# Zero columns added to the matmuls of layer 0, a different number for each weight group, and one projection summed at other PSUM columns

## The chip, the core and the metric

The kernel runs as one program on one core of one Trainium2 chip. The metric is device time in microseconds (us) of one execution. Before the change two executions took 2308.03 and 2309.26 us, a median of 2308.65. A third execution, recorded by the hardware profiler, took 2307.92 us; its span from the first to the last instruction is 2306.1 us.

## What is computed

A decoder trunk of two layers over 272 tokens (16 learned prefix tokens and a sequence of 256), width 2048, 16 heads of 128, feed-forward width 8192, all in fp32. Layer 0 mixes tokens with forgetting attention, layer 1 with stick-breaking attention over one shared K/V. What matters here are the dense products; in the reference they are:

```python
h = jnp.concatenate([meta, x], axis=1)                    # 272 tokens
a = rms_norm(h, norm_attn[0])
proj = a @ fox_w_in[0]                                    # q, k, v, forget gates
h = h + o.reshape(b, length, D_MODEL) @ fox_w_o[0]        # o: forgetting attention
h = h + squared_relu_mlp(rms_norm(h, norm_mlp[0]), w_up[0], w_down[0])
a = rms_norm(h, norm_attn[1])
c = rms_norm(h, kv_norm)
k_s, v_s = jnp.split(c @ w_kv, 2, axis=-1)                # shared K/V, all 272 tokens
q = split_heads(a @ sb_w_q[0])
h = h + o.reshape(b, length, D_MODEL) @ sb_w_o[0]         # o: stick-breaking attention
h = h + squared_relu_mlp(rms_norm(h, norm_mlp[1]), w_up[1], w_down[1])
return rms_norm(h, final_norm)[:, N_META:]
```

## The kernel before

**Layout.** Activations lie feature-major: 16 chunks of 128 features on the partitions, tokens along the free axis. A layer-0 product works on 272 tokens, and so does the shared K/V projection; the rest of layer 1 works on the 256 tokens behind the prefix.

**A split operand.** Every dense product is made from fp32r matmuls. Each operand is split into a high part, which fp32r holds, and a low part with the remainder, and three products are summed: weight-high by x-high, weight-high by x-low, weight-low by x-high. The class `Split` allocates the x tile: per chunk 640 columns, with the high part starting at a column given by `ROWS` and the low part 320 columns behind it. The start is column 48 for the 272-token tiles and column 0 for the 256-token tiles. The pool `xs` holds two such tiles, so a new tile waits for the last reader of the one whose place it takes.

**A weight group.** `gemm_group` multiplies x by a 2048 x 512 block of weights. It allocates four PSUM tiles `acc` of one bank each (512 fp32 columns), one for each block m of 128 output features. The reduction runs in four steps kb of four chunks kc. For each kb two weight halves are loaded by SyncE's DMA queue, ScalarE writes the high part (`whi`, line 219) and VectorE the low part (`wlo`, line 220). Then come 48 matmuls per kb, 192 per group, each with a weight load of its own, all recorded at line 179 in the helper `gemm_matmul`. In layer 0 the order inside a kb is block by block (or in halves of a kb), and for each chunk the three products follow one another. In layer 1 the order is product by product across the blocks, and three of a group's 192 matmuls are 262 columns wide instead of 256: they read `sp.wide`, which goes six columns beyond x into zeros that GpSimd wrote from the tile `pad` (line 132).

**The groups in order.** They are numbered u by the order in which the code makes them: 1 to 12 are q, k and v of layer 0 in four rounds of four heads, 13 to 16 the output projection of layer 0, 17 to 48 its MLP, 49 to 52 the queries of layer 1, 53 to 60 the shared K/V, 61 to 64 the output projection of layer 1 and 65 to 96 its MLP. An MLP runs in four quarters f of the hidden width: four up groups that read `x_m` and write the quarter's hidden tile `x_u`, then four down groups that read that tile. For layer 0 this makes u = 17 + 8f + g, with g from 0 to 3 for the up groups and from 4 to 7 for the down groups.

**What sets the order.** A scheduler that simulates a timeline places the instructions on each engine's queue. Within the dense products the order of the matmuls is pinned by explicit dependencies from one to the next, except in the first group, whose x arrives piece by piece. The attention matmuls of a round are slotted between those of the next group. Each engine works through its queue in order.

**Lines.** `ROWS` and `Split` (lines 27 and 118 to 132), `gemm_group` (185 to 251), the matmul call (247) and the evacuation call (251). In attention, lines 295 and 296 multiply x by the 32 columns of the gate weights, 427 to 429 transpose probabilities into columns 0, 128 and 256 of one PSUM tile, 447 and 448 transpose packed values that GpSimd prepared at lines 338 and 345, and 588 to 593 are fp32r matmuls of 512 and 288 columns.

Of the kernel before, what the change touches and what calls it, by code (L numbers as in the profile page):

```python
# [15 lines left out]
P = 128  # L16
D = 2048
NC = D // P
M = 16
# [4 lines left out]
QSCALE = 1.0 / math.sqrt(P)  # L24
N_FF = 4

ROWS = {0: (48, 368), M: (0, 320)}
XROW = 640

G_A0, G_M0, G_KV, G_A1, G_M1, G_FIN = range(6)  # L30
# [3 lines left out]
def yoco_kernel(ctx: ExitStack, tc: tile.TileContext, hT_in, gains, b_f, w_f, w_qkv0, w_o0, w_up, w_dn,  # L34
                w_kv, w_q1, w_o1, outT):
    nc = tc.nc
# [77 lines left out]
    pad = align.tile([P, 32], F32, name="pad")  # L114
# [3 lines left out]
    class Split:  # L118


        def __init__(self, label, t0):
            n = T - t0
            self.t0 = t0
            rows = xs.tile([P, NC * XROW + 64], F32R, tag="x", name=f"x_{label}")
            hi, lo = ROWS[t0]
            rows = rows[:, hi:hi + NC * XROW].rearrange("p (c t) -> p c t", c=NC)
            d = lo - hi
            self.hi, self.lo = rows[:, :, :n], rows[:, :, d:d + n]
            if t0:

                self.wide = rows[:, :, :n + 6]
                nc.gpsimd.tensor_copy(rows[:, :, n:n + 6], pad[:, :6].unsqueeze(1).to_broadcast([P, NC, 6]))

    def split_chunk(sp, gi, c):

        g = g_sb[:, gi, c:c + 1]
        nc.scalar.activation(sp.hi[:, c], hT[:, c, sp.t0:], AF.Copy, scale=g)
        nc.vector.scalar_tensor_tensor(out=sp.lo[:, c], in0=hT[:, c, sp.t0:], scalar=g,
                                       in1=sp.hi[:, c].bitcast(F32), op0=ALU.mult, op1=ALU.subtract)
# [37 lines left out]
    def gemm_matmul(*args, **kw):  # L177

        ins = nc.tensor.matmul(*args, **kw).ins  # L179
        if queued and pinned[0]:  # L180
            tc.add_manual_dep(ins, queued[0].name, mybir.DependencyInfo(mybir.DependencyClass.NoSync,
                                                                        mybir.DependencyReason.DATA))
        queued[:] = [ins]

    def gemm_group(wblk, sp, t0, evac, before={}, after={}, load_x=None):

        uid[0] += 1
        u = uid[0]  # L190
        accs = [pacc.tile([P, 512], F32, tag="acc", name=f"acc_{u}_{m}") for m in range(4)]
        n = T - t0
        for kb in range(4):
            src_w = wblk[kb].rearrange("p (k c) -> p k c", k=4)
            if kb in before:
                before[kb]()
            piece = 1 if load_x is not None and kb < 2 else 2
            raws = [wraw.tile([P, 2, 512], F32, tag="raw", name=f"raw_{u}_{kb}_{hf}") for hf in range(2)]
            for k0 in range(0, 4, piece):
                if load_x is not None:  # L200
                    load_x(range(4 * kb + k0, 4 * kb + k0 + piece))
                if load_x is not None and kb == k0 == 0:

                    for c0 in (0, 256):
                        nc.scalar.dma_start(raws[0][:, 0, c0:c0 + 256], src_w[:, 0, c0:c0 + 256])
                else:
                    nc.sync.dma_start(raws[k0 // 2][:, k0 % 2:k0 % 2 + piece], src_w[:, k0:k0 + piece])
            parts = []
            for hf in range(2):
                whi, wlo = (wspl.tile([P, 2, 576], F32R, tag=f"w{x}", name=f"w{x}_{u}_{kb}_{hf}") for x in ("hi", "lo"))  # L210
                o = 16 if t0 else 0
                whi, wlo = whi[:, :, o:o + 512], wlo[:, :, o:o + 512]
                boxes = [(o, piece, 0, 512) for o in range(0, 2, piece)]
                if load_x is not None and kb == hf == 0:
                    boxes[:1] = [(0, 1, 0, 256), (0, 1, 256, 512)]
                for o, no, c0, c1 in boxes:
                    src = raws[hf][:, o:o + no, c0:c1]
                    hp, lp = whi[:, o:o + no, c0:c1], wlo[:, o:o + no, c0:c1]
                    on_act = nc.scalar.activation(hp, src, AF.Copy)  # L219
                    on_dve = nc.vector.tensor_tensor(out=lp, in0=src, in1=hp.bitcast(F32), op=ALU.subtract)  # L220
                parts.append((whi, wlo))
            if kb in after:
                with tc.issue_after(on_act.ins), tc.issue_after(on_dve.ins):
                    after[kb]()

            if load_x is not None and kb == 0:
                runs = [([kc], range(4)) for kc in range(4)]
            elif kb in (0, 3):
                runs = [(range(4), [m]) for m in range(4)]
            else:  # L230
                runs = [(range(2 * hf, 2 * hf + 2), range(4)) for hf in range(2)]
            pinned[0] = load_x is None
            for kcs, ms in runs:
                pairs = ((0, sp.hi), (0, sp.lo), (1, sp.hi))
                if t0:
                    products = [(kc, m, *pair) for pair in pairs for kc in kcs for m in ms]
                else:
                    products = [(kc, m, *pair) for m in ms for kc in kcs for pair in pairs]
                left = {m: 3 * len(kcs) for m in ms}

                wide = [(0, 0, 0), (1, 0, 1), (2, 1, 1)] if t0 else []
                for kc, m, part, x in products:
                    first, left[m] = kb == kc == 0 and left[m] == 3 * len(kcs), left[m] - 1
                    nw = n
                    if m == 3 and x is sp.hi and (kb, kc, part) in wide:
                        x, nw = sp.wide, n + 6
                    gemm_matmul(accs[m][:, :nw], parts[kc // 2][part][:, kc % 2, m * P:(m + 1) * P], x[:, 4 * kb + kc],
                                start=first, stop=kb == kc == 3 and left[m] == 0)
                if kb == 3:
                    for m in ms:  # L250
                        evac(m, accs[m][:, :n])

    def residual_add(c, acc, t0):
        nc.vector.tensor_tensor(out=hT[:, c, t0:], in0=acc, in1=hT[:, c, t0:], op=ALU.add)  # L254
# [6 lines left out]
    def load_x(chunks):  # L261
        c0, n = chunks[0], len(chunks)
        nc.sync.dma_start(hT[:, c0:c0 + n, :], hT_in[:, c0:c0 + n, :])
        if c0 == 0:
            nc.sync.dma_start(g_sb, gains)
        for c in chunks:
            split_chunk(xa, G_A0, c)
# [86 lines left out]
    for g in range(4):  # L354
# [11 lines left out]
        if g == 0:  # L366

            gemm_group(w_qkv0[0], xa, 0, lambda m, acc, qT=qT: nc.scalar.copy(qT[:, m, :], acc),
                       after={kb: (lambda kb=kb: first_norm(kb)) for kb in range(4)}, load_x=load_x)
            gate_products()  # L370
            box["rstd"] = norm.finish()
            for m in range(4):
                evac_q(m, qT[:, m, :])
            forget_gates(box["rstd"])
        else:
            gemm_group(w_qkv0[3 * g], xa, 0, evac_q)
# [4 lines left out]
        def decays(j):  # L381

            for i, (o, n) in enumerate(((0, 144), (144, T))):
                nc.vector.scalar_tensor_tensor(out=s[:, j, o:o + n], in0=fk[:, j, :n],
                                               scalar=fq_sb[:, i, 4 * g + j:4 * g + j + 1],
                                               in1=maskA[:, o:o + n], op0=ALU.subtract, op1=ALU.add)

        gemm_group(w_qkv0[3 * g + 1], xa, 0, lambda m, acc: evac_kv(m, acc, kT),
                   after={j: (lambda j=j: decays(j)) for j in range(4)})

# [263 lines left out]
    for i in range(2):  # L654
        pr = patt.tile([P, 512], F32, tag="patt", name=f"pr_fin_{i}")
        for b in range(2):
            nc.tensor.matmul(pr[:, b * P:(b + 1) * P], rs[:, b:b + 1].to_broadcast([P, P]), ident,
                             start=True, stop=True)
# [67 lines left out]
```

## Time and profile before

| what | value |
|---|---|
| median of two executions | 2308.65 us |
| profiled execution, its own time | 2307.92 us |
| its span, first to last instruction | 2306.1 us |
| TensorE clock granted, mean over the span | 0.998 of full |
| VectorE busy | 1290.2 us, 56% |
| ScalarE busy | 1041.7 us, 45% |
| GpSimd busy | 42.4 us, 2% |
| read from HBM | 407 MB, 178 GB/s over the span |

A row of the profile's groups gives line, engine, operation, output and inputs, the shape (stationary size, then output), a count, busy time, and the mean duration of one instruction. Matmuls overlap in a pipeline, so the mean duration of one (281 ns for most dense matmuls) is longer than the time from its start to the next one's start. That time is called the step in what follows, and it is read from rows of the timeline or of a window: the difference of two start times, divided by the matmuls started between them.

### The profile page before, as it was taken

To read this page: it belongs to the slowest core of one execution; us is meant where nothing else is said; L and a number is where in the kernel's file an instruction comes from. 1 tells how busy PE (TensorE), PEld (TensorE's weight loads), DVE (VectorE), ACT (ScalarE), POOL (GpSimd) and SP (SyncE) were. 2 spreads that over 40 slices of the span, in tenths; PEclk is the share of its full clock that TensorE was granted. 3 is DMA by queue.
4 is the path that set the end of the run, shared out by engine and by line. 5 is a ranking of instruction groups with operands and counts; after the bars stand their busy time and mean duration, and the time that the engine had idled before them with its cause. 6 is when DMAs were issued, how large, how long until landed. Compare 5 with 4: busy or idle time off the path is not lost.

```text
span 2306.1 us, 44831 instructions
## 1 busy us (share of the span) xinstructions
PE 2294.4 (99%) x19030; PEld 2281.9 (99%) x19030; DVE 1290.2 (56%) x1764; ACT 1041.7 (45%) x1397; POOL 42.4 (2%) x65
## 2 busy tenths in 40 slices
PE   9999999999999999999999999999999999999998
PEld 9999999999999999999999999999999999999998
DVE  7665555655455455455566555566555555555554
ACT  6444344543344344345444444455543543543553
POOL 1010000000000000000000000000000000000000
PEclk9999999999999999999999999999999999999999
DMA  7544445555555555555556444456556556566563
GB/s 239 169 156 167 166 165 167 172 183 177 180 174 181 180 171 186 177 181 170 186 180 200 161 144 146 146 167 199 186 192 203 186 195 201 184 201 197 188 200 130
DMA packets 116648, 412.32 MB, mean 179 GB/s; under 512 B 13264, under 2 KB 16736, under 8 KB 116448
## 3 DMA queue, kind: packets, MB, share of 16 engines
q1 hardware_dynamic: 114560, 406.29, 52.9%
q8 instruction: 149, 2.44, 0.4%
q10 hardware_dynamic: 1888, 3.16, 0.4%
q14 instruction: 51, 0.42, 0.1%
HBM read 407.29 MB, written 2.11 MB: 178 GB/s over the span
## 4 chain that ended last, share of the span: by engine, by line
PE 99%; DVE 0%; DMA 0%; ACT 0%; SPq 0%; issue 0%; DVEq 0%; ACTq 0%
PE acc L179 95%; PE ps L396 0%; PE pza L573 0%; PE pv L329 0%; PE po L458 0%; PE po L612 0%; DMA raw<-w_qkv 0%; PE po L613 0%; PE pzb L574 0%; PE po L459 0%; PE po L614 0%; DVE ob L668 0%; PE pf L295 0%; PE pf L296 0%; PE pta L588 0%; PE pta L589 0%
## 5 line engine op out<-in xcount | busy, mean ns | idle before, releaser
L220 DVE TENSOR_TENSOR wlo<-raw,whi 128x1024 fp32r<-128x1024 f32 (+1 forms) x773 | 928.2, 1217 | 752.6 <-ACT whi L219 745.9
L219 ACT ACTIVATE whi<-raw 128x1024 fp32r<-128x1024 f32 (+1 forms) x773 | 796.5, 1050 | 999.0 <-PE acc L179 984.3
L179 PE MATMUL acc<-x_m,whi 128*128 128x272 f32 (+1 forms) x4096 | 643.1, 281 | 0.0
L179 PE MATMUL acc<-x_u,whi 128*128 128x272 f32 (+1 forms) x4096 | 643.0, 281 | 0.0
L179 PEld LDWEIGHTS acc<-x_m,whi 128*128 128x128 f32 x4096 | 566.1, 188 | 0.1
L179 PEld LDWEIGHTS acc<-x_u,whi 128*128 128x128 f32 x4096 | 566.0, 188 | 0.0
L179 PE MATMUL acc<-x_u,wlo 128*128 128x272 f32 (+2 forms) x2048 | 440.8, 281 | 0.0
L179 PE MATMUL acc<-x_m,wlo 128*128 128x272 f32 (+2 forms) x2048 | 440.8, 281 | 0.0
L179 PE MATMUL acc<-x_a,whi 128*128 128x272 f32 (+1 forms) x2048 | 359.6, 288 | 0.7 <-ACT whi L219 0.6
L179 PEld LDWEIGHTS acc<-x_m,wlo 128*128 128x128 f32 x2048 | 323.3, 188 | 0.0
L179 PEld LDWEIGHTS acc<-x_u,wlo 128*128 128x128 f32 x2048 | 323.3, 188 | 0.0
L179 PEld LDWEIGHTS acc<-x_a,whi 128*128 128x128 f32 x2048 | 301.3, 188 | 2.9 <-ACT whi L219 0.8
L179 PE MATMUL acc<-x_a,wlo 128*128 128x272 f32 (+2 forms) x1024 | 253.7, 285 | 0.0
L179 PE MATMUL acc<-x_kv,whi 128*128 128x272 f32 x1024 | 194.1, 288 | 0.0
L179 PEld LDWEIGHTS acc<-x_a,wlo 128*128 128x128 f32 x1024 | 175.6, 188 | 0.7 <-issue 0.5
L179 PE MATMUL acc<-x_o,whi 128*128 128x272 f32 (+1 forms) x1024 | 162.3, 282 | 0.0
L179 PEld LDWEIGHTS acc<-x_kv,whi 128*128 128x128 f32 x1024 | 160.6, 188 | 0.4
L179 PE MATMUL acc<-x_kv,wlo 128*128 128x272 f32 x512 | 147.3, 288 | 0.0
L179 PEld LDWEIGHTS acc<-x_o,whi 128*128 128x128 f32 x1024 | 142.0, 188 | 0.1
L254 DVE TENSOR_TENSOR hT<-acc,hT 128x272 f32<-128x272 f32 (+1 forms) x160 | 69.1, 432 | 84.8 <-PE acc L179 84.6
L179 PE MATMUL acc<-x_o,wlo 128*128 128x272 f32 (+2 forms) x512 | 110.6, 282 | 0.0
L179 PEld LDWEIGHTS acc<-x_kv,wlo 128*128 128x128 f32 x512 | 96.5, 188 | 0.1
(225 smaller groups left out, 972.4 us busy)
## 6 DMA issues: line engine op xcount, KB each, us to landing
raw<-w_up SPq DMA_DIRECT2D x256, 512.0 KB, 4.6
raw<-w_dn SPq DMA_DIRECT2D x256, 512.0 KB, 4.5
raw<-w_qkv SPq DMA_DIRECT2D x92, 512.0 KB, 3.7
raw<-w_o SPq DMA_DIRECT2D x64, 512.0 KB, 4.2
raw<-w_kv SPq DMA_DIRECT2D x64, 512.0 KB, 3.8
raw<-w_q SPq DMA_DIRECT2D x32, 512.0 KB, 4.8
fk<-f_dram ACTq DMA_DIRECT2D x4, 544.0 KB, 5.1
raw<-w_qkv SPq DMA_DIRECT2D x7, 256.0 KB, 4.6
```

The lines of the kernel that those rows point to most:

```text
L179: ins = nc.tensor.matmul(*args, **kw).ins
L219: on_act = nc.scalar.activation(hp, src, AF.Copy)
L220: on_dve = nc.vector.tensor_tensor(out=lp, in0=src, in1=hp.bitcast(F32), op=ALU.subtract)
L254: nc.vector.tensor_tensor(out=hT[:, c, t0:], in0=acc, in1=hT[:, c, t0:], op=ALU.add)
```

## The change

`ROWS` is now looked up by the label of the tile. The layer-0 tiles and `kv` stay at column 48 but for the hidden tiles of quarters 1, 2 and 3, which start at columns 0, 16 and 32; the tiles of layer 1 are where they were. Each 272-token tile gets 30 columns of zeros behind the high part and behind the low part of each chunk, from GpSimd: two copies of 16 x 30 columns for each of eight tiles.

A matmul of a 272-token group now reads nw columns, 272 plus a number from `zeros`, and writes as many columns of the bank. What `zeros` gives:

- groups 1 to 12 and 53 to 60: 2 to 24 columns (2, 4, ... 24 in groups 1 to 12, then 10, 12, ... 24 in groups 53 to 60), but in three of the 192 matmuls only: the first one into block 3, and the weight-low product of chunk 3, block 3 in the first two steps kb;
- groups 13 to 16: none, but their sums lie from column 16, 64, 128 and 240 of the bank;
- up groups of the layer-0 MLP: 8f + 2g columns in all 192 matmuls, so 0, 2, 4, 6 in quarter 0 up to 24, 26, 28, 30 in quarter 3;
- its down groups: 0, 4, 8 and 12 columns in all 192 matmuls, in every quarter.

The added columns hold zeros, and the evacuation reads the same 272 columns as before, so no output changes.

```diff
-ROWS = {0: (48, 368), M: (0, 320)}
+ROWS = {"a0": (48, 368), "kv": (48, 368), "o0": (48, 368), "m0": (48, 368), "u0_0": (48, 368), "u0_1": (0, 320),
+        "u0_2": (16, 336), "u0_3": (32, 352),
+        "a1": (0, 320), "o1": (0, 320), "m1": (0, 320), "u1_0": (0, 320), "u1_1": (0, 320),
+        "u1_2": (0, 320), "u1_3": (0, 320)}
+
+def zeros(u, kb, kc, m, k):
+    if 1 <= u <= 12 or 53 <= u <= 60:
+        return 2 * ((u - 1) % 12) + 2 if (kc, m, k) == (3, 3, 2) and kb in (0, 1) else 0
+    if u <= 16:
+        return 0
+    if u <= 48:
+        f, g = divmod(u - 17, 8)
+        return 8 * f + 2 * g if g < 4 else 4 * (g - 4)
+    return 0
...
-            hi, lo = ROWS[t0]
+            hi, lo = ROWS[label]
...
+            else:
+                self.rows = rows
+                for o in (0, d):
+                    nc.gpsimd.tensor_copy(rows[:, :, o + n:o + n + 30], pad[:, :30].unsqueeze(1).to_broadcast([P, NC, 30]))
...
+                    if t0 == 0:
+                        off = (16, 64, 128, 240)[u - 13] if 13 <= u <= 16 else 0
+                        k = 2 if part else 1 if x is sp.lo else 0
+                        single = u <= 12 or 53 <= u <= 60
+                        nw = n + (zeros(u, 0, 3, 3, 2) if single and first and m == 3 else zeros(u, kb, kc, m, k))
+                        o = 320 if k == 1 else 0
+                        gemm_matmul(accs[m][:, off:off + nw], parts[kc // 2][part][:, kc % 2, m * P:(m + 1) * P],
+                                    sp.rows[:, 4 * kb + kc, o:o + nw], start=first, stop=kb == kc == 3 and left[m] == 0)
+                        continue
...
-                        evac(m, accs[m][:, :n])
+                        off = (16, 64, 128, 240)[u - 13] if 13 <= u <= 16 else 0
+                        evac(m, accs[m][:, off:off + n])
```

## The prediction, made before the changed kernel had run

> **What bounds the kernel now.** I read the page first, then the windows by stage, then the timeline of TensorE at places where matmuls of different widths stand side by side.
>
> ```profile
> PE 2294.4 (99%) x19030; PEld 2281.9 (99%) x19030; DVE 1290.2 (56%) x1764; ACT 1041.7 (45%) x1397; POOL 42.4 (2%) x65
> PE 99%; DVE 0%; DMA 0%; ACT 0%; SPq 0%; issue 0%; DVEq 0%; ACTq 0%
> 429.20:1187.40 758.20, 758.20 (x6148) 1.00 0.53 178
> 348.20:372.86 24.66, 24.66 (x202) 1.00 0.53 170
> ```
>
> The first line is the busy time of each engine, the second the chain of waits by engine: TensorE works 99% of the span and carries 99% of the chain. The other two rows are windows: length, TensorE busy time and instructions that touch the window, granted clock, DMA share, GB/s. The MLP of layer 0 (groups 17 to 48) fills 758.20 us without a gap: 32 x 192 = 6144 dense matmuls, two records of a norm and two that began before the window, so a step of about 123.3 ns. The other row, just behind a stretch in which attention matmuls interrupted the output projection, has 200 matmuls started in 24.66 us: 123.3 ns again. VectorE and ScalarE are at about half, DMA is busy for 0.53 of the time, and the clock is full. So the time changes by what a step of TensorE changes by, times the steps; nothing else is close to being late, and slower matmuls make it less so.
>
> **What a column costs.** No 274- to 302-column matmul is in this trace. These are:
>
> ```profile
> 1237.02 1.98 PE L179 MATMUL acc<-x_a,whi 128*128 128x256 f32 x16
> ...
> 1242.46 1.98 PE L179 MATMUL acc<-x_a,whi 128*128 128x256 f32 x16
> ...
> 1517.64 1.11 PE L179 MATMUL acc<-x_o,wlo 128*128 128x256 f32 x8
> ...
> 1521.41 2.00 PE L179 MATMUL acc<-x_o,whi 128*128 128x256 f32 x16
> 1523.25 1.07 PE L179 MATMUL acc<-x_o,wlo 128*128 128x256 f32 x8
> 1524.16 1.07 PE L179 MATMUL acc<-x_o,whi 128*128 128x256 f32 x8
> ...
> 1329.83 0.40 PE L588 MATMUL pta<-eh,ntri_r 128*128 128x512 f32 x1
> 1330.06 0.29 PE L592 MATMUL ptb<-eh,ntri_r 128*128 128x288 f32 x1
> 1331.18 0.40 PE L589 MATMUL pta<-el,ntri_r 128*128 128x512 f32 x1
> 1331.42 0.29 PE L590 MATMUL pta<-eh,nones_r 128*128 128x288 f32 x1
> 1331.55 0.30 PE L591 MATMUL pta<-el,nones_r 128*128 128x288 f32 x1
> 1331.68 0.29 PE L593 MATMUL ptb<-el,ntri_r 128*128 128x288 f32 x1
> ```
>
> Columns: start, length, instruction, count. A 512-column fp32r matmul is followed by the next after 0.23 and 0.24 us. Against the 272-column step, 240 columns more cost (235 - 123.3) / 240 = 0.465 ns each, 0.445 if the shorter one is taken. A 288-column matmul takes 130 ns, 0.42 ns a column above 272. A 256-column matmul has two steps in this trace. In group 50, 48 of them go from 1237.02 to 1242.46: 113.3 ns. In group 61, behind an interruption, 32 go from 1517.64 to 1521.41: 117.8 ns, and a little later, once the group's 262-column matmul has passed, 8 go from 1523.25 to 1524.16: 113.8 ns. So the same instruction on the same addresses has a slow and a fast step, 4.5 ns apart, and a wider matmul between them seems to move it from one to the other. From these two, a column between 256 and 272 costs (123.3 - 117.8) / 16 = 0.34 ns or (123.3 - 113.3) / 16 = 0.625 ns: the bounds. I take 0.45 ns, by the 512-column rows, which have the widest base and lie on the same side of 272 as the change.
>
> The Trainium skill, page "TensorE: Matmul & The Clock Gate", section "Back-to-back issue gap", gives an isolated warm matmul N/2.4 + 2.5 ns, so 0.417 ns a column, and 115.8 ns at 272; the rows show 123.3 at 272, so the page is too low for fp32r here, and by it the widening below would be 26.9 us instead of 29.0.
>
> **The sum, part by part.**
>
> The layer-0 MLP, all matmuls of a group widened. Columns added by group: up 0+2+4+6, 8+10+12+14, 16+18+20+22, 24+26+28+30, which is 240; down 0+4+8+12 four times, which is 96. 336 x 192 = 64,512 columns, times 0.45 ns: **29.0 us**; bounds 21.9 (0.34) and 40.3 (0.625). It is all on the path, since the window has no gap.
>
> The single widened matmuls. Groups 1 to 12 add 2 to 24 columns, together 156, groups 53 to 60 10 to 24, together 136; three matmuls each: 876 columns, **0.4 us** (0.3 to 0.5).
>
> The state of the step. Scaled to 272 columns, the two steps at 256 would be 113.3 x 272/256 = 120.4 ns and 125.2 ns; the real one, 123.3, lies between. Another width, another start column in the x tile (0, 16 or 32 in place of 48) or a single wide matmul may move a group to either: -2.9 or +1.9 ns a matmul. 30 of the 32 MLP groups are touched, 5760 matmuls: -16.7 to +10.9 us. The 20 groups with single widenings have 3840: -11.1 to +7.3 us. I take **0** for both, by the nearest row: the window behind the interruption. An interruption kicks the sequence harder than a column more or less, and at 272 columns the step is 123.3 behind it as it is elsewhere, so at this width I see one state, not two.
>
> The sums of groups 13 to 16 at columns 16, 64, 128 and 240:
>
> ```profile
> L429 PE MATMUL pp<-ident,s 128*128 128x128 f32 x16 | 4.4, 272 | 0.0
> L428 PE MATMUL pp<-ident,s 128*128 128x128 f32 x16 | 4.3, 272 | 0.0
> L427 PE MATMUL pp<-ident,s 128*128 128x128 f32 x16 | 4.3, 271 | 0.0
> ```
>
> These write columns 0, 128 and 256 of one bank and take 271, 272 and 272 ns: the place in the bank costs **0**. They are not fp32r and their mean is a duration, so as bounds I keep the same -2.9 and +1.9 ns for 768 matmuls: -2.2 to +1.5 us.
>
> The zeros that GpSimd writes, 16 copies of 480 elements a partition:
>
> ```profile
> L132 POOL CAST x_a<-pad 128x96 fp32r<-128x96 f32 x1 | 0.3, 269 | 759.5 <-PE acc L179 759.5
> L338 POOL COPY pk_qm<-qT 128x64 f32<-128x64 f32 x4 | 9.8, 2451 | 113.5 <-DVE qT L360 113.5
> 4.60 0.49 POOL L109 TENSOR_SCALAR_AFFINE_SELECT maskD<-maskD 128x128 f32<-128x128 f32 x1
> 7.32 1.26 PE L179 MATMUL acc<-x_a,whi 128*128 128x272 f32 x8 [0.58 <-ACT whi L219]
> 8.42 0.66 PE L179 MATMUL acc<-x_a,wlo 128*128 128x272 f32 x4
> 330.84 1.22 POOL L338 COPY pk_vm<-vT 128x128 f32<-128x128 f32 x1 [20.09 <-DVE vT L364]
> 333.84 0.27 PE L447 MATMUL pvm<-ident,pk_vm 128*128 128x128 f32 x1
> ```
>
> The same copy of 96 elements takes 0.269 us, so 480 take at most five times that, 1.35 us; a GpSimd copy of another kind took 2.45 us, the upper bound. Two places have a reader soon behind them. In the first group, the first matmul into block 3 reads zeros and now waits for GpSimd. In the changed program it stands 19th among the dense matmuls instead of 4th, and the two copies stand right behind the mask that ends at 5.09 us: done by 7.8 us, or 10.0 at the bound. The 19th matmul was at about 8.1 us (13th at 7.32, 21st at 8.42), so 0, up to 1.9 us at the bound; behind it the rest of the first step kb would queue. The other place is round 3 of attention: the zeros of `x_m` now stand on GpSimd's queue ahead of the packed copy that ended at 332.06 us and was first read at 333.84. That read stands 25 matmuls later in the changed program, 3.1 us, and two copies are 2.7 us: hidden, 0.1 us late at the bound. The six other tiles are written one to four groups (23.7 us each) ahead of their first reader. Cover holds: **0**, at most 2.0 us. The other moves of the scheduler swap neighbours on ScalarE and VectorE, which are not late.
>
> Sum: 29.0 + 0.4 + 0 = 29.4 us on the profiled execution's own 2307.9 us (span 2306.1 and 1.8 around it): 2337.3. The median of the runs, 2308.65, lies 0.7 above that execution, so **2338 us**, 1.3% longer.
>
> **Rivals.**
>
> *A fast step for the taking (not slower).* If the added columns bring the groups to the fast step, as a 262-column matmul does at 256, then with the cheap column: 21.9 + 0.3 - 16.7 - 11.1 - 2.2 = -7.8, so 2301 us. With columns at 0.45 it breaks even where 29.4 us are spread over all 10,368 matmuls that the change reaches, 2.8 ns each, so nearly every group must get there. For it speaks that two states exist at 256; against it, the single state at 272 and that three widened matmuls a group already follow many kinds of interruption. Chance 0.08.
>
> *Columns hidden by the weight load.* Were a step set by the 128-column weight load and not by the columns, widening would be free: 2309 us.
>
> ```profile
> 30.76 0.28 PE L296 MATMUL pf<-x_a,wf 128*32 128x272 f32 x1
> ...
> 33.49 0.29 PE L296 MATMUL pf<-x_a,wf 128*32 128x272 f32 x1
> ```
>
> Between these two rows the gate products run alternately, 22 steps in 2.73 us: 124.1 ns with a weight load of 32 columns, the same as with 128. And 512 columns do cost more. Chance 0.03. The same page of the Trainium skill and section give a sustained stream 81 ns a matmul at 128 columns and 131 at 512, which is 0.13 ns a column and would make 8.4 us of the widening; the 0.23 us of the 512-column rows here speak against it.
>
> *Dear columns or the slow step (slower by over 2%).* Columns at 0.625, groups at the slow step, the copies late: 2308.7 + 40.3 + 0.5 + 10.9 + 7.3 + 1.5 + 2.0 = 2371 us. The 2% line, at 2355 us, is passed when the MLP's state term and column price bring 46 us together, 7.5 ns more a matmul than now. A start column that makes the read of x slower than any row here would do it too. Chance 0.09.
>
> *The main case*, columns at about 0.45 and no change of state over all, single groups a few ns off: 0.80.
>
> **How the numbers follow.** The main case alone spans 2338 with the column at 0.34 to 0.5 and a third of the state term either way, about 2322 to 2348. To hold the time 8 times in 10 the range also takes part of the rivals: 2316 to 2354. A measurement here can tell about 2% from no change. Faster by over 2% needs below 2262, which even the first rival's low end does not reach: 0.01. Slower by over 2%: 0.07, most of the dear case. Within 2%: 0.92.
>
> **What would show it.** In the profile after, the layer-0 MLP window, 758.2 us now, should be about 787 long. Its groups should step by 123.3 ns plus 0.45 ns for each added column: up group 44, with 30 columns, 136.8 ns, down groups of 12 columns 128.7. Groups of no added columns in quarters 1 to 3 show what the start column does alone, groups 13 to 16 the PSUM column alone: both 123.3. The windows of groups 1 to 12 and 53 to 60 should be as long as now. I am wrong if the steps jump between neighbouring widths by several ns rather than rise along a line, if single wide matmuls change the step of the matmuls behind them, or if TensorE waits for GpSimd at 8 us.

## The result, and where the time went

The changed kernel takes 2350.21 us (two executions, 2349.92 and 2350.50) against 2308.65 us: a ratio of 1.0178, 95% interval 1.0157 to 1.0198. That is 41.6 us more, where 29.4 were forecast. Its profiled execution took 2349.92 us, its span is 2348.2 us. The page's busy times and its chain by engine:

```profile
PE 2336.4 (99%) x19030; PEld 2323.6 (99%) x19030; DVE 1292.6 (55%) x1764; ACT 1041.9 (44%) x1397; POOL 55.2 (2%) x81
...
PE 99%; DMA 0%; DVE 0%; ACT 0%; SPq 0%; issue 0%; DVEq 0%; ACTq 0%
```

TensorE's busy time has grown by 42.0 us, the span by 42.1. GpSimd has 12.8 us more work, the zeros, VectorE 2.4 and ScalarE 0.2, and the chain holds next to nothing of any of them. The same stretches of both kernels as windows, before and then after: groups 2 to 12, 13 to 16, and 53 to 60 (the layer-0 MLP of before is in the prediction; taken from the first matmul of group 17 to that of group 49 it is 758.23 us).

```profile
33.61:330.13 296.52, 296.52 (x2344) 1.00 0.48 165
330.13:429.19 99.06, 99.06 (x802) 1.00 0.51 171
...
1275.13:1501.75 226.62, 226.62 (x1756) 1.00 0.44 149
```

```profile
34.44:331.27 296.83, 296.83 (x2345) 1.00 0.51 164
331.27:430.32 99.05, 99.05 (x802) 1.00 0.54 171
430.32:1228.98 798.66, 798.66 (x6148) 1.00 0.53 169
1316.70:1543.71 227.01, 227.01 (x1756) 1.00 0.46 149
```

The MLP of layer 0 holds 40.4 us of the 42.1, groups 2 to 12 and 53 to 60 together 0.7, group 1 and the start before it 0.8, the moved PSUM columns nothing. Now single groups of the changed kernel, each from its first matmul to the next group's; the length divided by 192 is the step:

```profile
454.46:478.78 24.32, 24.32 (x195) 1.00 0.53 173
527.84:551.53 23.69, 23.69 (x195) 1.00 0.55 179
...
600.50:626.09 25.59, 25.59 (x194) 1.00 0.50 165
...
701.27:725.60 24.33, 24.33 (x195) 1.00 0.55 174
725.60:749.66 24.06, 24.06 (x194) 1.00 0.56 176
926.52:950.84 24.32, 24.32 (x195) 1.00 0.55 173
...
1024.51:1051.36 26.85, 26.85 (x194) 1.00 0.49 157
1103.85:1130.31 26.46, 26.46 (x194) 1.00 0.51 160
```

In order: group 18 (274 columns) 126.7 ns, 21 (272) 123.4, 24 (284) 133.3, 28 (286) 126.7, 29 (272, x tile at column 0) 125.3, 37 (272, at 16) 126.7, 41 (296) 139.8, 44 (302) 137.8. A step does grow with the width, by 14.4 ns over 30 columns. But it jumps by 3.3 ns with the first two columns, 286 columns are 6.6 ns faster than 284, 302 faster than 296, and the groups with a moved x tile are slower without any added column.

### The profile page after: what moved, and what is told of

Its sections match the earlier page's. It is cut to its first block, busy times and chain, and to the rows that moved or that the text cites. A ratio compares the mean times of both kernels' runs of the same rounds, so it can differ in the third digit from the quotient of the medians.

```text
span 2348.2 us, 44853 instructions
## 1 busy us (share of the span) xinstructions
PE 2336.4 (99%) x19030; PEld 2323.6 (99%) x19030; DVE 1292.6 (55%) x1764; ACT 1041.9 (44%) x1397; POOL 55.2 (2%) x81
## 4 chain that ended last, share of the span: by engine, by line
PE 99%; DMA 0%; DVE 0%; ACT 0%; SPq 0%; issue 0%; DVEq 0%; ACTq 0%
PE acc L201 96%; PE ps L428 0%; PE pza L605 0%; PE pv L361 0%; PE po L490 0%; PE po L644 0%; DMA raw<-w_qkv 0%; PE pzb L606 0%; PE po L645 0%; PE po L491 0%; PE po L646 0%; DVE ob L700 0%; PE pf L328 0%; PE pf L327 0%; PE pta L620 0%; PE pta L621 0%
## 5 line engine op out<-in xcount | busy, mean ns | idle before, releaser
L201 PE MATMUL acc<-x_m,whi 128*128 128x256 f32 (+16 forms) x4096 | 669.5, 285 | 0.0
L201 PE MATMUL acc<-x_u,whi 128*128 128x256 f32 (+4 forms) x4096 | 656.8, 283 | 0.0
L201 PEld LDWEIGHTS acc<-x_m,whi 128*128 128x128 f32 x4096 | 575.1, 188 | 0.1
L201 PE MATMUL acc<-x_m,wlo 128*128 128x256 f32 (+17 forms) x2048 | 448.7, 285 | 0.0
L201 PE MATMUL acc<-x_u,wlo 128*128 128x256 f32 (+5 forms) x2048 | 444.7, 283 | 0.0
L201 PE MATMUL acc<-x_a,whi 128*128 128x272 f32 (+2 forms) x2048 | 360.5, 288 | 0.9 <-ACT whi L241 0.6
L201 PE MATMUL acc<-x_a,wlo 128*128 128x272 f32 (+3 forms) x1024 | 254.3, 286 | 0.0
L201 PE MATMUL acc<-x_kv,whi 128*128 128x272 f32 (+1 forms) x1024 | 194.5, 288 | 0.0
L201 PE MATMUL acc<-x_kv,wlo 128*128 128x272 f32 (+2 forms) x512 | 147.4, 288 | 0.0
```

## The experiments

Each is named by its main edit; times are medians, and the kernel before, run beside them on the same chip, took 2308.62 to 2309.68 us. None has groups 13 to 16 at other PSUM columns, and none but e8 has single wide matmuls in layer 0. The code under each gives its edit in short, not line for line. Two theories were set out first. A: 272 columns were cheap because the read of x, from column 48, ends at 320, a multiple of 64. B: width and start of the read each shift the step, and the end plays no part. A third, C, came with the second experiment: what counts is where x is read in relation to where the weights are read.

**Zeros ahead of the tokens (e1).**

```diff
-sp.rows[:, 4 * kb + kc, o:o + nw]            # x at 48, read to 320 + w
+sp.rows[:, 4 * kb + kc, 30 + o - w:30 + o + n]   # rows from column 18: read from 48 - w to 320
```

> The same number of added columns in each group of the layer-0 MLP, but the zeros stand ahead of the 272 tokens instead of behind them, so that every read of x ends at tile column 320 as before the change; all tiles start at column 48 again, no single widenings, no moved PSUM columns. Theory A (the 272-column step of 123.3 ns is cheap because the read ends at a multiple of 64 columns): no jump at the first two columns, steps on a line from 123.3 with about 0.45 ns a column, group 18 at 124.2, group 44 at 137; the MLP window of layer 0 about 29 us longer than the 758.2 before. Theory B (width and first column of the read each shift the step by a few ns, and the end plays no part of its own): steps scatter around the line by 2 to 4 ns as in the changed kernel, group 18 near 126.6; the window 35 to 42 us longer.

Measured 2351.72 us. Its groups 18, 24, 28 and 44, and the MLP window:

```profile
454.62:478.94 24.32, 24.32 (x194) 1.00 0.53 173
601.46:627.04 25.58, 25.58 (x194) 1.00 0.50 165
702.54:727.93 25.39, 25.39 (x194) 1.00 0.53 167
...
1105.39:1132.26 26.87, 26.87 (x194) 1.00 0.49 158
430.48:1230.45 799.97, 799.97 (x6149) 1.00 0.52 169
```

126.7, 133.2, 132.2 and 139.9 ns: the jump at two columns is there though the read ends at 320, and the window is 41.7 us longer. Theory A falls. 286 columns, cheap in the changed kernel, are dear here, so the width alone does not set the step either.

**Weight tiles at other columns (e2).** No column is added; `o` is where a weight tile starts in its 576 columns.

```diff
-                o = 16 if t0 else 0
+                o = 16 if t0 else (16 * f + 4 * g if g < 4 else 16 * (g - 4))   # MLP of layer 0; x_u at 48, 0, 16, 32
```

> No added columns at all; the x tiles of the MLP quarters start at columns 48, 0, 16 and 32, and the weight tiles of the up groups start at column 0, 4, 8 to 60, of the down groups at 0, 16, 32 and 48. Theory C (the step depends on where the weight load reads in relation to where the matmul reads): up groups, all with x at 48, vary by 2 to 4 ns with the weights' column, and down groups with the same difference between the two columns have the same step. Theory B (only the matmul's own read counts): all up groups at 123.3; down groups 123.3 in quarter 0, 125.3 in quarter 1, 126.7 in quarters 2 and 3, whatever the weights' column; the MLP window 758.2 + 6.6 = 765 us.

Measured 2323.22 us. Groups 20 (x at 48, weights at 12), 30 (x at 0, weights at 16), 39 (16 and 32), 48 (32 and 48), 21 (48 and 0) and the MLP window:

```profile
502.17:526.49 24.32, 24.32 (x194) 1.00 0.54 173
743.58:767.27 23.69, 23.69 (x195) 1.00 0.54 178
...
960.89:985.21 24.32, 24.32 (x194) 1.00 0.53 173
1178.93:1202.61 23.68, 23.68 (x194) 1.00 0.54 178
526.49:550.18 23.69, 23.69 (x194) 1.00 0.55 179
430.03:1202.61 772.58, 772.58 (x6148) 1.00 0.54 175
```

Group 20 reads the same x in the same way as before the change, only its weights lie 12 columns further, and its step is 126.7 instead of 123.3 ns. Groups 30, 48 and 21 share the difference 48 (column of x minus column of the weights, modulo 64) and all step by 123.3 to 123.4 ns, though x at 0 took 125.3 with its weights at 0. In 15 of the 16 down groups the step follows the difference. The exception is group 39, difference 48 and yet 126.7 ns. Theory B as written falls, C holds but for one group. The Trainium skill, page "TensorE: Matmul & The Clock Gate", section "Step-by-step: what each phase is for", says that loading the next tile's weights takes no SBUF read bandwidth from the running matmul, through a read port of its own; moving only the weights here costs 3.3 ns a matmul, so the stream is not free of where its weights are read. Whether a shared read makes it so, no run shows.

**The order of the matmuls (e3).** No added columns.

```diff
-products = [(kc, m, *pair) for m in ms for kc in kcs for pair in pairs]
+products = [(kc, m, *pair) for pair in pairs for kc in kcs for m in ms]                          # quarter 0
+products = [(kc, m, *pair) for m in ms for kc in kcs for pair in (pairs[0], pairs[2], pairs[1])] # quarter 1
+products = [(kc, m, *pair) for m in ms for pair in pairs for kc in kcs]                          # quarter 2
```

> No added columns, every tile of layer 0 at column 48; the order of the matmuls inside an MLP group differs by quarter: 0 product by product as in layer 1, 1 block by block with both products of x-high first, 2 block by block and product by product, 3 as before. If the step at 272 columns depends on which operand changes from one matmul to the next, quarters 0 to 2 leave 123.3 by 2 ns or more, up or down (to 120.4 if the fast step of layer 1 comes with its order); if only width and columns count, all quarters stay at 123.3 and the time equals that before the change.

Measured 2308.66 us against 2308.68 (ratio 1.0001, interval 0.9989 to 1.0012). A group of quarter 0, one of quarter 2, and the MLP window:

```profile
453.40:477.08 23.68, 23.68 (x195) 1.00 0.56 178
...
832.28:855.96 23.68, 23.68 (x195) 1.00 0.55 179
429.25:1187.48 758.23, 758.23 (x6148) 1.00 0.55 178
```

Both at 123.3 ns, and the window is that of before: at this width and this place of the two tiles the order plays no part, and the order of layer 1 alone brings no faster step.

**A fixed width and a sliding start (e4).**

```diff
+    w, w1 = (16, 2 * j) if j < 9 else (8, 2 * (j - 9)) if j < 14 else (4, 4 * (j - 14))   # w added, w1 of them ahead
+ROWS of x_u in quarters 0 to 3: 40, 24, 8, 56; no added columns in down groups
```

> Up groups: a fixed width and a sliding start. 288 columns starting at 48, 46, 44 to 32 (zeros move from behind to ahead), then 280 columns starting at 48 to 40, then 276 at 48 and 44. Down groups: 272 columns, x tiles starting at 40, 24, 8 and 56. Theory A: 288 columns are cheap (about 130.5 ns) only where the read ends at 320, that is at start 32, and 133 or more elsewhere; likewise 280 at start 40 and 276 at 44; the down groups, which end at 312, 296, 280 and 328, are all at about 126. Theory B: the step changes by several ns from one start to the next with no special place for an end at 320, and the down groups lie anywhere from 120.4 to 126.7.

Measured 2341.71 us. Group 20 (288 columns from 42), 33 (288 from 32, ending at 320), and the down groups 21, 29, 37 and 45 (272 from 40, 24, 8 and 56):

```profile
508.33:533.30 24.97, 24.97 (x195) 1.00 0.52 169
827.57:853.17 25.60, 25.60 (x194) 1.00 0.50 164
...
533.30:556.98 23.68, 23.68 (x195) 1.00 0.54 179
730.29:754.61 24.32, 24.32 (x194) 1.00 0.54 173
928.14:952.27 24.13, 24.13 (x194) 1.00 0.55 175
1123.25:1147.56 24.31, 24.31 (x195) 1.00 0.54 174
```

288 columns take 133.3 ns where the read ends at 320, and 130.1 from column 42; over the nine starts from 48 down to 32 the step goes 133.3 (group 17, outside the norm that interrupts it), 133.3, 131.4, 130.1, 133.3, 133.4, 130.0, 136.0, 133.3. 280 and 276 columns are no cheaper where the read ends at 320 either: 130.0 and 127.4 ns there, 128.3 and 126.7 from column 48. The down groups, with weights at 0, take 123.3, 126.7, 125.7 and 126.6 ns. The up groups of e2 in which x stayed at 48 and the weights moved to the same differences (40, 24, 8, 56) took 123.3, 126.6, 125.8 and 126.7. At these differences, moving x by some columns or the weights by as many the other way is the same thing.

**Weights that follow x (e7).** The changed kernel's widths and x columns, but the down groups' weight tiles moved along.

```diff
+    return (0, 8 * f + 2 * g, 0, 0) if g < 4 else (0, 4 * (g - 4), 0, (0, 16, 32, 48)[f])   # last: weight column
```

> The changed kernel's added columns in every MLP group of layer 0 and its start columns 48, 0, 16 and 32 of the hidden tiles, but in the down groups of quarters 1 to 3 the weight tiles start at 16, 32 and 48, so that the difference between x's and the weights' column is 48 as in quarter 0 (modulo 64); no single widenings, no moved PSUM columns. If the difference alone counts (with the width): the down groups of quarters 1 to 3 take the steps of quarter 0, 123.3, 126.7, 128.4 to 128.9 and 133.3 ns for 0, 4, 8 and 12 columns; up groups as in the changed kernel; the MLP window stays within 0.5 us of its 798.7. If x's own start column counts: the down groups keep the changed kernel's steps, 125.3 and 126.7 ns without added columns.

Measured 2349.06 us. Groups 29, 32, 37 and 45, and the MLP window:

```profile
725.25:748.94 23.69, 23.69 (x195) 1.00 0.55 178
...
797.90:823.07 25.17, 25.17 (x194) 1.00 0.51 168
926.11:949.80 23.69, 23.69 (x194) 1.00 0.55 178
1130.18:1153.86 23.68, 23.68 (x194) 1.00 0.58 178
429.97:1228.43 798.46, 798.46 (x6149) 1.00 0.52 169
```

The window is 0.2 us shorter than the changed kernel's. Groups 29, 37 and 45, with x at 0, 16 and 32 and no added columns, are back at 123.4, from 125.3, 126.7 and 126.7. All down groups have the steps of quarter 0 but group 32, which takes 131.1 instead of 133.3 ns at 284 columns. The sum hardly moves, because the differences that the changed kernel had in quarters 1 to 3 were worse at 272 columns and, taken together, better at 276 to 284. The 16 up groups have the same widths and places as in the changed kernel, and each has the same step there within 0.1 ns: the jumps from width to width are no scatter between executions.

**Every other difference at 272 columns (e5, e10), and one product alone (e6).** The column of the weight tiles in the first two, and the columns of x-low and weight-low alone in the third; x-high stays at 48.

```diff
+e5:  o = 16 * f + 4 * g + 2 if g < 4 else 16 * f + 4 * (g - 4) + 1
+e10: o = 16 * f + 4 * g + 3 if g < 4 else 0
+e6:  o = 0 for weight-high; 16 * f + 4 * g if g < 4 else (0, 16, 32, 8)[g - 4] for weight-low
+e6:  x_u of quarters 0 to 3 at (48, 48 + 320 + d), d = -16, 16, -32, 8
```

> No added columns, all x tiles at column 48; the weight tiles of the up groups start at column 2, 6, 10 to 62, of the down groups at 1, 5, 9 to 61. If the difference between the columns where x and the weights are read sets the step in multiples of 8 columns, as the runs so far suggest (123.3, 125 to 125.8 and 126.7 ns), these groups show the same three levels and none below 123.3, so the MLP window is 8 to 18 us longer than 758.2. Rival: an untried difference gives the equivalent of the fast step of layer 1, about 120 ns, so single groups are 0.6 us shorter than before.

> No added columns, all x tiles at column 48; the weight tiles of the up groups start at 3, 7, 11 to 63, those of the down groups at 0 as before. With the runs so far this makes all 64 differences of the two columns at a width of 272. If 123.3 ns is the lowest step of this width, no up group goes below it and the MLP window is 4 to 10 us longer than 758.2; if one of these differences gives the equivalent of the fast step of layer 1, that group steps by about 120 ns, and a kernel with that difference throughout would beat the one before. The down groups, at 123.3, show whether a group keeps what the group ahead of it left.

> No added columns, x-high and the weight-high tiles stay at columns 48 and 0. Up groups: the weight-low tile starts at column 0, 4, 8 to 60. Down groups: x-low is moved by -16, 16, -32 and 8 columns (one value a quarter) and weight-low by 0, 16, 32 and 8. If each matmul's own difference of columns sets its step, a group in which one of three products leaves difference 48 has a third of the loss seen when all three leave it: up to 124.4 ns instead of 126.7, and two of three up to 125.6. Rival: what counts is the weight load that runs beside the matmul, which belongs to the next product, so other groups of the table pay, and a group may come out above 126.7 or below 123.3.

Measured 2321.17, 2315.46 and 2320.24 us. From the second, group 19 (weights at 11), the slowest of all:

```profile
477.94:502.76 24.82, 24.82 (x194) 1.00 0.51 170
```

With these all 64 differences have been run at 272 columns. The steps go from 123.3 to 129.3 ns; none is lower than 123.3, so none of these differences, as they ran here, beats the kernel before. That kernel had difference 48 in both layers: its weight tiles start at column 0 in layer 0 and at 16 in layer 1 (`o = 16 if t0 else 0`), where x starts at 48 and at 0. The second expectation holds, its window being 6.1 us longer, and all its down groups step by 123.3 or 123.4 behind up groups of up to 129.3 ns: at this place a group keeps nothing of the group ahead. Of the first, the sum holds (11.9 us) and the three levels don't: several groups lie between them, 124.5 ns for one. In the third, groups 18 and 19, in which weight-low alone moved, by 4 and by 8 columns, and then group 19 of e2, in which both weight tiles start at column 8:

```profile
453.25:477.56 24.31, 24.31 (x194) 1.00 0.53 173
477.56:501.68 24.12, 24.12 (x195) 1.00 0.54 175
```

```profile
478.49:502.17 23.68, 23.68 (x194) 1.00 0.55 179
```

Group 18 takes 126.6 ns, the full loss, where one of three products was to give 124.4 at most. Group 19 takes 125.6, though with all three products at that difference it lost nothing (123.3). In 14 of the 32 groups the step is 124.4 to 124.5 ns, about a third of the full loss. So a matmul's own pair of columns does not always set its step. Either its neighbours in the stream count, as the rival has it, or these groups are in the other of two states (see e8); no run separates the two.

**Single wide matmuls (e8).** The kernel e2 with one more edit, and zeros behind x-high for the wide matmuls to read:

```diff
-wide = [(0, 0, 0), (1, 0, 1), (2, 1, 1)] if t0 else []                    # layer 1 alone
+wide = [(0, 0, 0), (1, 0, 1), (2, 1, 1)] if t0 or 17 <= u <= 48 else []
```

> The kernel with moved x tiles and weight tiles and no added columns (e2), and in each MLP group of layer 0 three matmuls that are 6 columns wider, as the groups of layer 1 have them. In e2 group 39 (difference 48) stepped by 126.7 ns, while groups of the same difference stepped by 123.3. If that group sat in another state that it had come into by chance, and a single wider matmul can move a group from one state to the other, group 39 goes to 123.3 behind its first or second wide matmul, other groups may change level too, and the MLP window differs from the 772.6 us of e2 by more than 1 us. If single wide matmuls do nothing at 272 columns, as in the changed kernel's groups 1 to 12, every group keeps its step of e2 and the window stays within 0.3 us of 772.6.

Measured 2322.17 us. Group 39, then group 44 up to its first wide matmul (36 steps) and behind it (154 steps), then group 39 up to its first wide matmul (36 steps):

```profile
960.35:984.08 23.73, 23.73 (x195) 1.00 0.54 177
```

```profile
1080.77:1085.33 4.56, 4.56 (x38) 1.00 0.34 110
1085.59:1104.76 19.17, 19.17 (x156) 1.00 0.59 193
960.35:964.80 4.45, 4.45 (x39) 1.00 0.33 114
```

Group 39 goes from 126.7 to 123.6 ns with the wide matmuls in it, 27 from 126.6 to 125.7 and 44 from 126.7 to 124.9; groups 19, 28 and 36 change in part, the other 26 keep their step. So some pairs of width and difference have two states. Group 44 shows that a single wider matmul can change the state: it steps by 126.7 ns up to its first wide matmul and by 124.5 behind it, where in e2 it steps by 126.7 throughout. Group 39 does not show that, against what was expected: it steps by 123.6 ns ahead of its own first wide matmul already, so it came into that state at its start, and what set it is open. The window is shorter by 0.85 us, under the 1 us that was expected.

**284 and 286 columns (e9).** x at 48 and weights at 0 throughout.

```diff
-        return 8 * f + 2 * g if g < 4 else 4 * (g - 4)
+        return 12 if g < 4 else 14
```

> All up groups of the layer-0 MLP 284 columns wide, all down groups 286, x tiles at column 48 and weights at 0. A price by the column (0.45 ns): 128.7 and 129.6 ns, the MLP window 3072 x (5.4 + 6.3) ns = 36 us longer than 758.2. By the single groups of the changed kernel, where 284 columns took 133.3 and 286 took 126.7: 3072 x (10.0 + 3.4) ns = 41 us longer, and the wider groups are the faster ones. If a group's step hangs on the state that the group before left, single groups of one width differ.

Measured 2350.08 us. An up group, a down group, the MLP window:

```profile
507.25:532.85 25.60, 25.60 (x195) 1.00 0.51 165
532.85:557.18 24.33, 24.33 (x194) 1.00 0.53 174
430.00:1229.18 799.18, 799.18 (x6148) 1.00 0.52 169
```

Sixteen groups at 133.3 (group 17 outside the norm that interrupts it) and sixteen at 126.7 ns, 41.0 us in all, as the changed kernel's single groups said and not as a price by the column said. Two more columns make a matmul 6.6 ns faster here, every time.

## Why the prediction was right, and where its sum was short

**The range** held, but in part by luck. The 2350 us lie above the 2322 to 2348 that the main case alone was to span, in the room that the range took from the dear rival. And the first of the prediction's own signs of being wrong came: the steps jump between neighbouring widths, 284 to 286 columns by 6.6 ns downward, instead of rising along a line.

**The bound** was right: TensorE's stream sets the time, and nothing took its place.

**The MLP.** The direction, the place and the size of the trend were right: from 272 to 302 columns at difference 48 the step rises by 0.48 ns a column, near the 0.45 taken. A line fitted through the steps of the 18 widened groups with that difference, up and down, has 0.44 ns a column (an estimate from the group windows of the changed kernel's trace). But it meets 272 columns at 125.5 ns and not at 123.3, and single groups lie from 5.0 ns below it to 3.7 above.

So what was mis-sized is the state of the step, taken as 0 with an upper bound of 10.9 us. The MLP lost 40.4 us, and 29.0 of it at 0.45 ns a column, so 11.4 us are left for that term, 1.9 of them if the column is taken at 0.48. Over the 5760 matmuls touched that is 2.0 ns each, the slow end of the term. The moved x tiles are not what makes up the 11.4 us: groups 29, 37 and 45, with no column added, lose 0.38, 0.64 and 0.64 us, but with every group at difference 48 (e7) 11.2 of the 11.4 us are still there. They come with the added columns, of which the first two can already cost 3.3 ns. The row that 0 was taken from, the steady 123.3 ns behind an interruption, was true, but only of 272 columns at the place the two tiles had, and a steady step there says nothing of the next width.

Over 64 differences, 123.3 is the lowest step that any run here shows for 272 columns, so any move of x alone could only keep it or lose. So for groups that only move x the sign of the term was not open, as the prediction had it. Among the widened groups one did reach the low end: group 28, at 126.7 ns, where the line from 123.3 has 129.6 for 286 columns. The group steps named ahead were short in the same way: group 44 was to take 136.8 ns and took 137.8, 12-column down groups 128.7 and took 130.3 to 133.3, and group 18, by the same price, 124.2 and took 126.7. One label is off: the 48 matmuls from 1237.02 us, called group 50, are of group 51; their 113.3 ns stand.

**The single wide matmuls** were to cost 0.4 us and cost 0.7 in groups 2 to 12 and 53 to 60. That they change no state there, at 272 columns and difference 48, was right; that 272 columns have one state was not, as group 39, of the same difference, shows in e2 and e8.

**The PSUM columns** cost nothing: 99.06 us before, 99.05 after.

**The zeros on GpSimd** were hidden at both places, by the margins that had been given. GpSimd and TensorE of the changed kernel; two copies of `x_a` run one after the other, then those of `x_o`:

```profile
4.89 1.51 POOL L154 CAST x_a<-pad 128x480 fp32r<-128x480 f32 x2
...
331.57 2.12 POOL L154 CAST x_m<-pad 128x480 fp32r<-128x480 f32 x2 [19.53 <-PE acc L201]
333.64 1.28 POOL L370 COPY pk_vm<-vT 128x128 f32<-128x128 f32 x1
```

```profile
8.96 0.42 PE L201 MATMUL acc<-x_a,whi 128*128 128x274 f32 x2
...
338.05 0.27 PE L479 MATMUL pvm<-ident,pk_vm 128*128 128x128 f32 x1
```

The first copies end at 6.40 us, and the matmul that reads them starts at 8.96 without an idle time before it; the second pair delays the packed copy to 334.92 us, read at 338.05. Group 1 took 0.7 us longer than before, but 0.8 longer in e2, which writes no zeros behind the layer-0 tiles; so that is not put down to the change.

**The rivals.** The fast step did not come: no run shows a 272-column step below 123.3 ns. Hidden columns are out, as the widened MLP lost 40.4 us. Of the dear case, the state term of the MLP came whole (11.4 us, or 9.5 with the column at 0.48, against 10.9), with the column price of the main case. All 40.4 us put on the columns would be 0.63 ns each, the upper bound of the column price; that the fitted line does not pass through 123.3 speaks against this reading.

What stays open is what in the machine makes the step depend on the two columns modulo 64 and jump with the width, whether a matmul's neighbours in the stream share in it, and what puts a group into one of two states; no run separated a read, a port or a queue. Weight loads of fewer columns in the dense stream were not tried.

## What to carry to other kernels

Where a stream of matmuls with a weight load each is the bound, the step can hang on the width and on the relative place of the two operands together, as it did here. Measure the width and the layout that are meant to be used, since a line drawn through other widths was off here by up to 6 ns a matmul. And before pricing a change of layout as "either way", find out whether the present one is already the best of its kind: then it can only lose.

## What the runs showed that was not expected

- The weights' place matters as much as x's: 12 columns more for the weights alone took a 272-column step from 123.3 to 126.7 ns. Moving either tile to the same difference modulo 64 columns gave the same step within 0.1 ns in the four differences that were run both ways (8, 24, 40, 56).
- Many steps lie on multiples of 3.33 ns (123.3, 126.7, 130.0, 133.3, 136.7, 140.0), so a few columns more can cost nothing or a whole notch, and in e9 286 columns lie two notches below 284.
